# Norms and gates that read the matmul's PSUM bank directly, in a two-layer decoder trunk on one core

## The chip, the cores and the metric

The kernel runs on one core of one Trainium2 chip. The core has five engines that run side by side, each through its own queue of instructions: TensorE (PE in the profile; its weight loads are listed as PEld), VectorE (DVE), ScalarE (ACT), GpSimd (POOL) and SyncE (SP), which issues the DMAs. Matmuls write PSUM, which has eight banks of 128x512 float32; VectorE and ScalarE read PSUM, GpSimd in this kernel works on SBUF only.

The metric is the time of one execution in device microseconds, the median of several runs. Lower is better.

## The reference

Two residual layers over 1024 tokens of width 1024. Each layer normalises its input, projects it with one wide weight matrix, runs three mixers on slices of the projection, multiplies each mixer's output by its own gate, and projects back:

```python
h = rms_norm(x, ln_g[layer])
u = h @ w_in[layer]                       # even: 2,744 columns, odd: 3,504
y1, y2, y_m = mixers(split_cols(u))       # even: latent attention | sparse block attention | memory attention
                                          # odd:  indexer-selected attention | mLSTM | memory attention
mix = concat([y1 * silu(gate1), y2 * silu(gate2), y_m * silu(gate_m)])
x = x + mix @ w_out[layer]
```

Almost every slice of `u` that becomes a query or a key is normalised head by head before use: `rms_norm(q) = q * rsqrt(mean(q*q) + 1e-6) * g`. In the indexer-selected attention each query attends to the 256 keys with the highest index scores; the index scores come from eight small index queries per token. For the first 256 tokens every earlier key is among the 256, so their index queries decide nothing.

## The kernel before

All work is on tiles of 128 tokens (`NT = 8`). A float32 matrix product is made of three float16 products of high and low halves (`mm3`, line 1061). The float16 halves of a weight block are scaled by a power of two; undoing that scale is a multiplication by a per-partition column `wi[:, 0:1]` (`winv` in the profile), which every consumer of a projection does while it copies the result from PSUM.

- `load_w` (979) loads a weight block in pages, squares each page for a sum (`wj`, `wss`), adds the pages' sums with a reduction (`wst`), sums over partitions with a float32 matmul against a matrix of ones, and derives the power-of-two scale. It then makes the halves `wl`.
- `project` (1071) runs over the blocks of a layer and the eight tiles: 24 matmuls per tile and block of up to 512 columns into one PSUM bank (`psO`), then a `post` function on that bank.
- A normalising `post` (`q_post`, `k_rope`, `post_lat`, `mem_post`, `kv_post` of `mla_kv`, `q_post` of `mla_q`, `post_idx`) makes two passes over the bank: a scaled copy into SBUF (tiles `qu`, `ku`, `lu`, `mqu`, `kvk`, `xu`) and a ScalarE square with the same scale. The rest uses SBUF: VectorE sums the squares, `rstd` (785) makes mean plus epsilon, GpSimd raises it to the power -0.5 (`rsqrt`, 781), and a multiply applies it to the copy. That multiply goes through `tt` (777), which may run on VectorE or GpSimd.
- A gate (`gate_post`, 1334; `post_og`, 2157) makes a tanh (`gth`, `ogt`) and a scaled copy (`gu`, `ogu`), both from the bank, and `silu` (1346) combines them on VectorE: (tanh + 1) * copy.

Nothing of this runs in program order. A recorder notes every operation with its dependencies; a planner (`order`, line 303) then lists, for each engine, the order in which its operations are issued. Operations are ranked by a key: each section of the program has an interval in the table `SEG`, and its operations are spread over that interval. Operations recorded through `copy` may run on ScalarE or VectorE, those through `tt` on VectorE or GpSimd (in the odd or out-projection parts a few other sets). The planner gives such an operation to the engine with the smallest estimated finish, in which `PRICE` weights each engine's duration (line 356):

```python
fin = {x: max(te[x], ready(o, x), shared(o, x), room) + alt[3] * (1 + PRICE[x]) for x, alt in o.alts.items()}
```

It also hands out the eight PSUM banks, which attention (`psS`, two banks for a unit of scores; `psT`, `psO`) shares with the projections. Attention per unit of work: scores into PSUM, a maximum (`nm`, VectorE), the exponential (`P` or `psum`, ScalarE), a split into two float16 halves (`PS` or `PT`: a scaled copy on either engine, then a subtraction on VectorE), a transpose by DMA or TensorE, and the product with the values.

Of the kernel before, what the change touches and what calls it, by code (L numbers as in the profile page):

```python
# [25 lines left out]
PRICE = {"V": 0.0, "S": 0.0, "G": 0.0}  # L26
# [636 lines left out]
def shape_constants():  # L663
# [8 lines left out]
    for i in range(NT):  # L672
# [8 lines left out]
SEG = dict(setup=(-1576.69593, -601.132494), mem1=(-688.598351, 20.410205), e_agate=(30.600801, 726.724683), norm=(40.663363,  # L681
           43.886871), kv0=(144.84029, 484.056211), late=(244.088906, 537.79462), cmp=(419.157656, 678.361546), nsak=(441.736796,
           1111.702063), nsav=(473.744964, 852.150721), q1=(516.97553, 589.82681), e_kv1=(657.175124, 658.175124), e_lat=(663.1,
           841.289575), q0=(716.011325, 958.711325), e_bgate=(717.414855, 785.212098), kv1=(721.080648, 931.480648), e_bq=(743.2,
           988.9), e_mq=(765.062608, 934.79172), e_kv2=(784.700952, 841.5), nsa=(850.7, 1310.2), mla0=(911.5, 1001.5),
           mla1=(949.844544, 1032.244544), mem0=(995.320402, 1196.998026), tab1=(998.505496, 1809.787053), oA0=(1017.297313,
           1145.595371), mkv0=(1037.7, 1137.062), oBM0=(1117.135472, 1369.183228), o_idx=(1295.192627, 1405.371644),
           topk0=(1315.598497, 1922.144632), o_og1=(1337.144784, 1596.707927), o_cgate=(1397.764817, 1813.702265),
           topk1=(1438.6657, 1890.616024), o_og0=(1538.232471, 1831.481071), o_dqk=(1661.136623, 1731.218797), o_mq=(1698.247094,
           1772.209632), o_cq=(1740.832086, 1897.126292), mlstm=(1752.857474, 2015.6), o_dv=(1791.594452, 1899.65152),  # L690
           mkv1=(1795.136495, 1846.39911), cv=(1864.304863, 1962.048226), dsa=(1918.765321, 2334.316374), oBM1=(1988.164978,
           2223.083031), oA1=(2187.593261, 2496.721847))
# [13 lines left out]
class Trunk:  # L706
    def __init__(self, tc, A, out, ctx):
# [19 lines left out]
        self.rec = rec = Recorder(LIMITS)  # L727
        self.real = dict(V=nc.vector, S=nc.scalar, G=nc.gpsimd, T=nc.tensor, Q=nc.sync)
        self.V, self.S, self.G, self.T, self.Q = (Engine(rec, n, self.real[n]) for n in "VSGTQ")

    soft = False
# [63 lines left out]
    def setup(self):  # L795
# [12 lines left out]
        V.memset(self.ones, 1.0)  # L808
        self.gmax = self.const([128, 6], F, "gmax")
# [169 lines left out]
    def load_w(self, parts, nk, gain=None, fuse=False):  # L979
# [91 lines left out]
    def project(self, layer, blocks, hT, gain):  # L1071

        for name, (parts, post) in blocks.items():
# [260 lines left out]
    def gate_post(self, dst, o=0):  # L1334
# [11 lines left out]
    def silu(self, out, th, u):  # L1346

        if self.soft:
            self.tt(th, th, u, OP.mult, "G")
# [1161 lines left out]
```

## Time and profile before

| | |
|---|---|
| median of 3 runs | 1514.36 us (1513.29 to 1518.81) |
| the profiled execution | 1524.7 us, of it 1522.9 us from the first to the last instruction |
| TensorE | 1397.5 us busy, 92%; granted clock 0.957 of full speed on average |
| VectorE | 1355.0 us, 89% |
| ScalarE | 1061.1 us, 70% |
| GpSimd | 380.2 us, 25% |

The profile cuts the span into stretches and gives each engine's busy time in each. Every operation carries one line number, that of the recorder's issue loop (L559), so groups are told apart by the names of the tiles they write and read: `qu<-psum,winv` is the scaled copy of a query block, `qu<-qu,ms` the multiply by the reciprocal root. A granted clock of 1.00 is 2.4 GHz, 0.50 is 1.2 GHz.

### The profile page before, as it was taken

To read this page: it belongs to the slowest core of one execution; us is meant where nothing else is said; L and a number is where in the kernel's file an instruction comes from. 1 tells how busy PE (TensorE), PEld (TensorE's weight loads), DVE (VectorE), ACT (ScalarE), POOL (GpSimd) and SP (SyncE) were. 2 spreads that over 40 slices of the span, in tenths; PEclk is the share of its full clock that TensorE was granted. 3 is DMA by queue.
4 is the path that set the end of the run, shared out by engine and by line. 5 is a ranking of instruction groups with operands and counts; after the bars stand their busy time and mean duration, and the time that the engine had idled before them with its cause. 6 is when DMAs were issued, how large, how long until landed. Compare 5 with 4: busy or idle time off the path is not lost. (4 is left out here: it accounts for less than half of the span.)

```text
span 1522.9 us, 29899 instructions
## 1 busy us (share of the span) xinstructions
PE 1397.5 (92%) x10407; PEld 796.4 (52%) x10407; DVE 1355.0 (89%) x3681; ACT 1061.1 (70%) x2460; POOL 380.2 (25%) x436
## 2 busy tenths in 40 slices
PE   4999999979898889979999999999989898999988
PEld 1445446546666555655565544444444445655554
DVE  7867989899999898899999989779999999799994
ACT  6733855578876787786777679999889824456561
POOL 1411344557520123341114100001222121210110
PEclk9999999989999999989999999999998899689999
DMA  9847222367884889878987404013242645459994
GB/s 295 198 147 173 94 82 84 92 150 165 142 175 103 188 198 235 229 165 176 231 194 167 116 23 139 15 56 97 67 125 80 129 87 170 112 133 263 266 222 142
DMA packets 441847, 225.47 MB, mean 148 GB/s; under 512 B 378080, under 2 KB 404320, under 8 KB 441696
## 3 DMA queue, kind: packets, MB, share of 16 engines
q1 hardware_dynamic: 441696, 223.57, 59.6%
q8 instruction: 81, 1.33, 0.4%
q14 instruction: 70, 0.57, 0.1%
HBM read 83.61 MB, written 46.66 MB: 86 GB/s over the span
## 5 line engine op out<-in xcount | busy, mean ns | idle before, releaser
L559 PE MATMUL psum<-wl,hT 128*128 128x512 f16 (+3 forms) x2880 | 680.9, 372 | 11.9 <-DVE wl L559 4.3
L559 PEld LDWEIGHTS <-hT 128*128 128x128 f16 x2880 | 276.9, 99 | 307.4 <-issue 34.2
L559 PEld LDWEIGHTS <-PT 128*128 128x128 f16 x3792 | 248.4, 103 | 66.4 <-DMA PT<-PS 27.1
L559 PE MATMUL psum<-wl,oT 128*128 128x512 f16 x960 | 273.8, 385 | 3.3 <-DMA oT<-osp 0.9
L559 POOL TENSOR_TENSOR ms<-ms,nhalf 128x4 f32<-128x4 f32 (+3 forms) x105 | 113.9, 1092 | 435.0 <-DVE ms L559 335.1
L559 PE MATMUL psum<-nv,PT 128*128 128x64 f16 x1584 | 183.3, 193 | 11.3 <-DMA PT<-PS 6.4
L559 ACT ACTIVATE psum<-psum,nm 128x256 f32<-128x256 f32 (+8 forms) x234 | 137.4, 591 | 68.1 <-DVE nm L559 53.4
L559 DVE TENSOR_REDUCE nm<-psum 128x2 f32<-128x512 f32 (+8 forms) x216 | 162.4, 764 | 19.7 <-PE psum L559 18.9
L559 PEld LDWEIGHTS <-oT 128*128 128x128 f16 x960 | 93.9, 99 | 100.3 <-issue 8.1
L559 ACT ACTIVATE P<-psum,nm 128x64 f32<-128x64 f32 (+8 forms) x150 | 92.4, 623 | 57.7 <-DVE nm L559 46.0
L559 DVE SCALAR_TENSOR_TENSOR PS<-psum,PS 128x512 f16<-128x512 f32 (+6 forms) x160 | 124.1, 783 | 2.5 <-ACT PS L559 2.4
L559 PE MATMUL psum<-cst,P 128*128 128x128 f32 x502 | 107.3, 299 | 10.9 <-DVE PS L559 6.8
L559 PEld LDWEIGHTS <-qf 128*128 128x128 f16 x832 | 78.6, 103 | 66.4 <-issue 23.1
L559 PE MATMUL psum<-cvp,PT 128*128 128x64 f16 x864 | 106.1, 200 | 5.6 <-DMA PT<-PS 5.6
L559 ACT ACTIVATE PT<-psum 128x512 f16<-128x512 f32 (+3 forms) x160 | 77.4, 505 | 45.4 <-PE psum L559 40.2
L559 PE MATMUL psum<-nkst,qf 128*128 128x320 f16 (+5 forms) x384 | 93.5, 322 | 3.9 <-DVE PS L559 2.1
L559 DVE TENSOR_TENSOR wl<-wr,wl 128x1024 f16<-128x1024 f32 (+4 forms) x76 | 92.8, 1230 | 0.8 <-ACT wl L559 0.5
L559 ACT ACTIVATE tkj<-tkr,tkv 128x384 bf16<-128x384 f32 (+5 forms) x96 | 83.8, 879 | 13.5 <-DVE tkv L559 7.5
L559 DVE SCALAR_TENSOR_TENSOR PT<-psum,PT 128x512 f16<-128x512 f32 (+3 forms) x160 | 88.2, 566 | 5.3 <-ACT PT L559 5.2
L559 PEld LDWEIGHTS psum<-cst,P 128*128 128x128 f32 x502 | 68.2, 145 | 31.0 <-DVE PS L559 7.6
L559 ACT ACTIVATE wj<-wr 128x1024 bf16<-128x1024 f32 (+6 forms) x73 | 74.1, 1020 | 13.7 <-DMA wr<-even_w_in 7.7
L559 ACT ACTIVATE tkj<-stop,tkd,tkf 128x768 bf16<-128x768 bf16 (+5 forms) x84 | 80.8, 970 | 0.4 <-DVE tkb L559 0.4
(508 smaller groups left out, 2896.1 us busy)
## 6 DMA issues: line engine op xcount, KB each, us to landing
wr<-even_w_in SPq DMA_DIRECT2D x20, 512.0 KB, 5.7
wr<-w_out SPq DMA_DIRECT2D x20, 512.0 KB, 5.4
wr<-odd_w_in SPq DMA_DIRECT2D x20, 512.0 KB, 4.3
gate<-gate_d SPq DMA_DIRECT2D x32, 256.0 KB, 4.2
gate_d<-gu SPq DMA_DIRECT2D x24, 256.0 KB, 2.1
qa_d<-mqT SPq DMA_DIRECT2D x16, 384.0 KB, 2.5
xt<-x SPq DMA_DIRECT2D x8, 512.0 KB, 9.9
x<-x SPq DMA_DIRECT2D x8, 512.0 KB, 5.3
```

Of the source, the lines that this page charges most:

```text
L559: r = getattr(engines[o.eng], meth)(*[res(a) for a in args], **{k: res(v) for k, v in kw.items()})
```

## The change

Four kinds of edits. First, the normalising posts and the gates no longer make the scaled copy: the square is taken of the unscaled bank, the epsilon is divided by the square of the scale (`eps_of`, two small VectorE operations per weight block), and the multiply reads the bank and runs on VectorE alone. The gates' scale is kept (`gw`) and multiplied once into a small per-head factor of the attention that the gate will multiply. Second, the weight sums go to the ones matmul in bfloat16, page by page. Third, for the first two token tiles the index projection leaves out the 256 columns of the index queries, in two column ranges instead of one. Fourth, `PRICE` and the table `SEG` have new numbers.

```diff
-PRICE = {"V": 0.0, "S": 0.0, "G": 0.0}
+PRICE = {"V": 0.715, "S": -0.1744, "G": 0.0874}
 ...
-SEG = dict(setup=(-1576.69593, -601.132494), mem1=(-688.598351, 20.410205), e_agate=(30.600801, 726.724683), ...
+SEG = dict(mem1=(-1888.036415, -777.253203), setup=(-1705.34707, -1400.274884), e_agate=(29.974308, 702.674675), ...
 ...
-    def rstd(self, ss, n, scale=1.0):
+    def rstd(self, ss, n, scale=1.0, eps=None):
         ms = self.tiny(ss.shape[-1], F, "ms")
         c2 = 1.0 / (scale * scale)
-        self.V.tensor_scalar(ms, ss, c2 / n, EPS * c2, op0=OP.mult, op1=OP.add)
+        self.V.tensor_scalar(ms, ss, c2 / n, EPS * c2 if eps is None else eps, op0=OP.mult, op1=OP.add)
         return self.rsqrt(ms)
+
+    def eps_of(self, w, c2=1.0):
+
+        key = (id(w.t), str(w.ops), c2)
+        if key not in self.epss:
+            e = self.tiny(2, F, "eps")
+            self.V.reciprocal(e[:, 0:1], w)
+            self.V.tensor_scalar(e[:, 1:2], e[:, 0:1], e[:, 0:1], EPS * c2, op0=OP.mult, op1=OP.mult)
+            self.epss[key] = (w, e[:, 1:2])
+        return self.epss[key][1]
 ...
-        tot = ss
-        if npg > 1:
-            tot = self.tiny(1, F, "wst")
-            V.tensor_reduce(out=tot, in_=ss, axis=AX.X, op=OP.add)
+        tot = self.tiny(npg, BF, "wst")
+        V.tensor_copy(tot, ss)
         gcols, gmax = self.gcols[gain]
         t = self.psT()
-        T.matmul(t[:, 0:1], self.ones, tot, start=True, stop=True)
+        for p in range(npg):
+            T.matmul(t[:, 0:1], self.oneb, tot[:, p:p + 1], start=p == 0, stop=p == npg - 1)
 ...
-                    self.mm3(ps[:, :n], [(hi[:, k], lo[:, k]) for k in range(8)], w)
+                    for a, b in (((0, 128), (384, n)) if name == "idx" and i < 2 else ((0, n),)):
+                        self.mm3(ps[:, a:b], [(hi[:, k], lo[:, k]) for k in range(8)], [(x[:, a:b], y[:, a:b]) for x, y in w])
 ...
-            th, u = self.page("gth", [128, n]), self.page("gu", [128, n])
-            self.S.activation(th, ps[:, o:o + n], AF.Tanh, scale=wi[:, 1:2])
-            self.copy(u, ps[:, o:o + n], scale=wi[:, 0:1])
-            self.silu(u, th, u)
+            if i == 0:
+                self.gw[name] = g = self.const([128, 1], F, "gw")
+                self.V.tensor_copy(g, wi[:, 0:1])
+            u = self.page("gu", [128, n])
+            self.S.activation(u, ps[:, o:o + n], AF.Tanh, scale=wi[:, 1:2])
+            self.silu(u, u, ps[:, o:o + n])
 ...
-        def norm_heads(u, sq, h, d, n, scale=1.0):
+        def norm_heads(u, src, sq, wi, h, d, n, scale=1.0):
+
+            S.activation(sq, src, AF.Square)
             ss = self.tiny(h, F, "nh")
-            V.tensor_reduce(out=ss, in_=sq.rearrange("p (h d) -> p h d", h=h), axis=AX.X, op=OP.add)
-            r = self.rstd(ss, n, scale)
-            u3 = u.rearrange("p (h d) -> p h d", h=h)
-            self.tt(u3, u3, self.bc(r, [128, h, d], 2), OP.mult)
-            return u3
+            h3 = lambda x: x.rearrange("p (h d) -> p h d", h=h)
+            V.tensor_reduce(out=ss, in_=h3(sq), axis=AX.X, op=OP.add)
+            r = self.rstd(ss, n, scale, self.eps_of(wi[:, 0:1], 1.0 / (scale * scale)))
+            V.tensor_tensor(out=h3(u), in0=h3(src), in1=self.bc(r, [128, h, d], 2), op=OP.mult)
+            return h3(u)
 ...
-                self.copy(u, ps, scale=wi[:, 0:1])
-                S.activation(sq, ps, AF.Square, scale=wi[:, 0:1])
-                u3 = norm_heads(u, sq, 8, 64, 64, 0.125)
+                u3 = norm_heads(u, ps, sq, wi, 8, 64, 64, 0.125)
 ...
+        V.tensor_scalar(inv, inv, self.gw["a"], None, op0=OP.mult)
 ...
+        for f in (cmp["inv"], vsi, vwi):
+            V.tensor_scalar(f, f, self.gw["b"], None, op0=OP.mult)
 ...
-                self.copy(u[:, 0], ps[:, 256:512], scale=wi[:, 0:1])
-                self.silu(u[:, 0], th[:, 1], u[:, 0])
+                self.silu(u[:, 0], th[:, 1], ps[:, 256:512])
                 self.silu(u[:, 1], th[:, 0], u[:, 0])
                 x3 = u[:, 1].rearrange("p (h d) -> p h d", h=2)
-                self.tt(x3, x3, hg, OP.mult)
+                V.scalar_tensor_tensor(out=x3, in0=x3, scalar=wi[:, 0:1], in1=hg, op0=OP.mult, op1=OP.mult)
```

`mem_post`, `k_rope`, `post_lat`, `kv_post`, `mla_q` and `post_idx` are changed in the way of `q_post` and `norm_heads`. `post_lat` makes its two float16 halves straight from the bank. All 36 intervals of `SEG` are new; the sections stay in much the same order, except that `mem1` now comes ahead of `setup`, `tab1` starts at 830 (998 before), `topk1` starts at 1272 (1439 before) and lies ahead of `topk0`.

## Rows read from the trace of the kernel before

**Rows 1.** Busy time by stretch: start:end, length, engines (instructions), clock, DMA share, GB/s
```profile
core 0: us, PE busy (x) PEld busy (x) DVE busy (x) ACT busy (x) POOL busy (x), PEclk, DMA share, GB/s
50.00:300.00 250.00, 249.99 (x1307) 130.25 (x1306) 208.04 (x757) 138.24 (x302) 89.78 (x89) 1.00 0.40 121
300.00:550.00 250.00, 212.93 (x2427) 147.41 (x2426) 237.85 (x546) 186.59 (x528) 95.41 (x129) 0.94 0.72 152
550.00:700.00 150.00, 131.96 (x1331) 85.17 (x1331) 138.96 (x311) 119.45 (x295) 53.05 (x51) 0.93 0.88 210
700.00:850.00 150.00, 144.49 (x1387) 89.29 (x1386) 142.37 (x334) 108.21 (x248) 33.98 (x56) 1.00 0.86 186
850.00:1000.00 150.00, 146.43 (x715) 70.35 (x714) 125.46 (x351) 132.33 (x259) 7.32 (x13) 0.99 0.24 76
1000.00:1150.00 150.00, 143.81 (x675) 67.11 (x673) 140.48 (x391) 136.25 (x285) 29.02 (x19) 0.99 0.30 86
1150.00:1350.00 200.00, 180.16 (x1096) 107.09 (x1096) 180.71 (x509) 116.66 (x312) 43.42 (x46) 0.84 0.46 115
1350.00:1500.00 150.00, 141.76 (x1281) 80.09 (x1280) 130.34 (x325) 85.36 (x176) 17.29 (x18) 0.98 0.96 230
```

**Rows 2.** Waits of TensorE, 300 to 550 us: who waited for whom, us, times, longest
```profile
PE psum L559 <- DVE PS L559: 10.1, 11, 2.3
PE psum L559 <- DMA PT<-PS: 7.7, 8, 1.9
PE psum L559 <- DVE PT L559: 4.0, 5, 1.6
PE psum L559 <- ACT P L559: 4.0, 3, 2.6
```

**Rows 3.** TensorE in order of time: start, us from first to last, instruction, count
```profile
809.90 0.90 PE L559 MATMUL psum<-wl,hT 128*128 128x432 f16 x4
1389.94 0.54 PE L559 MATMUL psum<-cvp,PT 128*128 128x64 f16 x13
43.14 0.28 PE L559 MATMUL psum<-wst,ones 128*128 128x1 f32 x2
43.28 0.92 PE L559 MATMUL psum<-wl,hT 128*128 128x512 f16 x3
```

**Rows 4.** Groups of scaled copies, whole span: count, busy us, mean ns, idle before
```profile
L559 DVE TENSOR_SCALAR gu<-psum,winv 128x512 f32<-128x512 f32 (+1 forms) x16 | 10.3, 644 | 2.8 <-PE psum L559 2.8
...
L559 DVE TENSOR_SCALAR qu<-psum,winv 128x512 f32<-128x512 f32 x3 | 2.2, 734 | 0.0
L559 ACT ACTIVATE gu<-psum,winv 128x512 f32<-128x512 f32 (+1 forms) x24 | 14.3, 597 | 2.3 <-DVE kvs L559 2.3
...
L559 ACT ACTIVATE xu<-psum,winv 128x416 f32<-128x416 f32 x4 | 2.4, 606 | 2.8 <-PE psum L559 2.8
```

**Rows 5.** Groups of multiplies and splits, whole span
```profile
L559 POOL TENSOR_TENSOR mqn<-mqu,mqms 128x256 f32<-128x256 f32 x4 | 2.6, 658 | 0.2
L559 DVE TENSOR_TENSOR mqn<-mqu,mqms 128x256 f32<-128x256 f32 x12 | 5.0, 414 | 0.7 <-POOL mqms L559 0.7
L559 DVE TENSOR_TENSOR mixA<-psum,cf 128x256 f32<-128x256 f32 x32 | 13.4, 418 | 4.3 <-PE psum L559 4.0
L559 DVE TENSOR_SCALAR gu<-psum,winv 128x256 f32<-128x256 f32 x6 | 2.9, 476 | 0.0
L559 DVE TENSOR_SCALAR lsp<-lu,lms 128x256 f16<-128x256 f32 x6 | 2.1, 346 | 0.0
L559 DVE TENSOR_REDUCE wst<-wss 128x1 f32<-128x4 f32 (+2 forms) x21 | 3.1, 146 | 1.9 <-ACT wj L559 1.9
```

**Rows 6.** Groups of movable operations on VectorE, 300 to 700 us, then 1150 to 1350
```profile
L559 DVE TENSOR_SCALAR PS<-psum 128x512 f16<-128x512 f32 (+6 forms) x34 | 27.9, 826 | 0.8 <-ACT psum L559 0.6
L559 DVE TENSOR_TENSOR wl<-wr,wl 128x1024 f16<-128x1024 f32 x9 | 11.5, 1274 | 0.2 <-ACT wl L559 0.2
L559 DVE TENSOR_SCALAR PS<-psum 128x512 f16<-128x512 f32 (+1 forms) x13 | 8.5, 663 | 0.5 <-ACT psum L559 0.5
L559 DVE TENSOR_TENSOR wl<-wr,wl 128x1024 f16<-128x1024 f32 x8 | 10.2, 1280 | 0.0
```

**Rows 7.** One query tile at 1258 us, in order of time: start, us, instruction, [idle before]
```profile
1258.14 0.70 ACT L559 ACTIVATE qsq<-psum,winv 128x512 f32<-128x512 f32 x1
1263.46 2.61 POOL L559 TENSOR_TENSOR ms<-ms,nhalf 128x8 f32<-128x8 f32 x2 [5.41 <-DVE ms L559]
1265.13 0.69 DVE L559 TENSOR_TENSOR qu<-qu,ms 128x512 f32<-128x512 f32 x1
```

More of the change, by code (lines that the diff above doesn't have):

```diff
@@ L678, in shape_constants @@
     return c
[L681 to L692, printed above, removed]
@@ new lines @@
+SEG = dict(mem1=(-1888.036415, -777.253203), setup=(-1705.34707, -1400.274884), e_agate=(29.974308, 702.674675), norm=(66.196882,
+           67.196882), kv0=(119.873601, 326.461801), late=(271.705755, 580.746202), nsak=(334.268778, 1740.215819),
+           cmp=(368.353292, 488.762377), nsav=(434.363812, 870.544721), q1=(475.175395, 617.189084), q0=(566.735709, 931.932049),
+           e_kv1=(660.555602, 663.443172), e_lat=(663.187987, 829.025091), e_bgate=(705.954963, 783.352092), kv1=(726.464295,
+           936.864295), e_bq=(737.259234, 982.959234), e_mq=(765.062608, 932.900552), e_kv2=(784.700952, 841.5), tab1=(830.090423,
+           1662.888056), nsa=(872.306006, 1326.817021), mla0=(909.091866, 999.091866), mla1=(969.44378, 1054.709671),
+           oA0=(1007.713145, 1135.977063), mkv0=(1040.445181, 1139.807181), mem0=(1079.69846, 1246.165943), oBM0=(1120.434423,
+           1372.482179), topk1=(1271.85213, 1873.537022), o_idx=(1296.691587, 1402.187939), topk0=(1324.470154, 1930.279265),
+           o_og1=(1349.453914, 1536.855486), o_cgate=(1379.693649, 1771.670217), o_og0=(1514.069868, 1768.540855),
+           o_dqk=(1600.358214, 1661.086999), o_mq=(1713.3677, 1855.898155), o_cq=(1753.414658, 1888.851314), o_dv=(1783.429201,
+           1908.616007), mlstm=(1817.611125, 2013.865219), cv=(1830.061497, 1982.44894), mkv1=(1844.716227, 1889.690991),
+           dsa=(1892.935508, 2303.398001), oBM1=(1962.41115, 2241.424255), oA1=(2195.850639, 2403.005228))
@@ L1346, in silu @@
     def silu(self, out, th, u):
-        if self.soft:
-            self.tt(th, th, u, OP.mult, "G")
-            self.tt(out, th, u, OP.add, "G")
-        else:
-            self.V.scalar_tensor_tensor(out=out, in0=th, scalar=1.0, in1=u, op0=OP.add, op1=OP.mult)
+        self.V.scalar_tensor_tensor(out=out, in0=th, scalar=1.0, in1=u, op0=OP.add, op1=OP.mult)
     def mem_kv(self, l):
@@ L1564, in post_lat @@
             pg = ptab[0]
-            u, sq = self.page("lu", [128, 416]), self.page("lsq", [128, 416])
-            self.copy(u, ps[:, 0:416], scale=wi[:, 0:1])
-            S.activation(sq, ps[:, 0:416], AF.Square, scale=wi[:, 0:1])
+            sq = self.page("lsq", [128, 416])
+            S.activation(sq, ps[:, 0:416], AF.Square)
             ss = self.tiny(3, F, "lss")
@@ L1573, in post_lat @@
             V.tensor_tensor(out=ms, in0=ss, in1=self.cst[:, C_MEAN:C_MEAN + 3], op=OP.mult)
-            V.tensor_scalar(ms, ms, EPS, None, op0=OP.add)
+            V.tensor_scalar(ms, ms, self.eps_of(wi[:, 0:1]), None, op0=OP.add)
             r = self.rsqrt(ms)
@@ L1734, in kv_post @@
             V.tensor_reduce(out=ss, in_=s4, axis=AX.X, op=OP.add)
-            r = self.rstd(ss, 64)
-            self.tt(k4, k4, self.bc(r, [128, 4, 64], 2), OP.mult)
+            r = self.tiny(4, F, "ms")
+            V.tensor_scalar(r, ss, bq[:, 1:2], self.eps_of(wk), op0=OP.mult, op1=OP.add)
+            self.rsqrt(r)
+            V.tensor_tensor(out=k4, in0=p4[:, :, 0:64], in1=self.bc(r, [128, 4, 64], 2), op=OP.mult)
             ks = self.split_rows(k4, "kvs")
@@ L1775, in q_post @@
         def q_post(i, ps):
-            u, sq = self.page("mqu", [128, 384]), self.page("mqs", [128, 384])
-            n = self.page("mqn", [128, 384])
-            self.copy(u, ps, scale=wi[:, 0:1])
-            S.activation(sq, ps, AF.Square, scale=wi[:, 0:1])
-            u4, s4 = h4(u), h4(sq)
+            sq, n = self.page("mqs", [128, 384]), self.page("mqn", [128, 384])
+            S.activation(sq, ps, AF.Square)
+            p4, s4 = h4(ps), h4(sq)
             ms = self.tiny(8, F, "mqms")
@@ L2003, in post_idx @@
             wv = wi[:, 0:1]
-            self.copy(u1[:, 0:416], ps[:, 0:416], scale=wv)
             self.copy(cv[:, i], ps[:, 64:128], scale=wv)
-            V.tensor_scalar(iw[:, i], ps[:, 416:424], wv, float(np.float32(8.0 ** -0.5)), op0=OP.mult, op1=OP.mult)
+            if i >= 2:
+                self.copy(u1[:, 128:416], ps[:, 128:416], scale=wv)
+                V.tensor_scalar(iw[:, i], ps[:, 416:424], wv, float(np.float32(8.0 ** -0.5)), op0=OP.mult, op1=OP.mult)
+            else:
+                self.copy(u1[:, 384:416], ps[:, 384:416], scale=wv)
             V.tensor_scalar(gif[:, i], ps[:, 424:432], wv, None, op0=OP.mult)
             sq = self.page("xsq", [128, 64])
-            S.activation(sq, ps[:, 0:64], AF.Square, scale=wv)
-            k3 = self.norm_heads(u1[:, 0:64], sq, 1, 64, 64)
+            k3 = self.norm_heads(u1[:, 0:64], ps[:, 0:64], sq, wi, 1, 64, 64)
             r = self.page("xr", [128, 8, 128])
@@ L2229, in dsa @@
         groups = []
+        V.tensor_scalar(vinv, vinv, self.gw["c"], None, op0=OP.mult)
         ql = self.q_load(cq_d, 128, 8)
```

51 lines of the change are left out of this document (27 added, 24 removed).

## The prediction

> **What bounds the kernel now.** I read the page first (TensorE 92% busy, VectorE 89%, ScalarE 70%, GpSimd 25%), then the busy time by stretch, since an average over stages hides which engine is the limit in each. [rows 1] show two kinds of stage. From 50 to 300 us TensorE is busy 249.99 of 250 us at clock 1.00: the projections of the even layer, bound by TensorE. From 700 to 1150 us it is busy 144 to 146 of 150 at clock 0.99 to 1.00: nearly so. From 300 to 700 us and from 1150 to 1350 us VectorE is the fullest engine (237.85 + 138.96 + 180.71 = 557.5 of 600 us), while TensorE is busy 525 of 600, and part of that at half clock: its clock of 0.94, 0.93 and 0.84 means that (0.06 x 250) + (0.07 x 150) + (0.16 x 200) = 57 us of full-speed work are lost, so at full clock it would need some 468 of 600. These 600 us are where VectorE's time counts. ScalarE is busy 423 of them, GpSimd 192. Who ends TensorE's waits there [rows 2]: VectorE 14.1 us (`PS`, `PT`), DMA 7.7, ScalarE 4.0. So VectorE ends 55% of the waits shown, no more.
>
> **The change part by part.**
>
> **Index columns.** Two tiles x 24 = 48 matmuls of 432 columns become 48 of 128 and 48 of 48. A run of four of 432 columns lasts 0.90 us from first start to last end [rows 3]; one lasts 0.35 by itself (the profile's matmul durations include the pipeline), so their spacing is about 0.55/3 = 0.183 us. Thirteen matmuls of 64 columns, each with a weight load of its own, last 0.54 us, 0.19 of it the last one's pipeline: 0.35/12 = 0.029 us apart. Then 128 columns cost 0.183 x 128/432 = 0.054, and the 48 no more than 0.029. Saved: 48 x (0.183 - 0.083) = **4.8 us**. The tiles lie near 810 us, in a stretch where TensorE is 96% busy, so I count all of it; bounds 0 and 4.8.
>
> **Weight sums.** The two passes of the float32 sum hold TensorE for 0.14 us: they start at 43.14, the next projection matmul at 43.28 [rows 3]. Four bfloat16 matmuls at 0.029 make 0.12. With 21 sums that is 0.5 us. The copy takes the place of a reduction of 146 ns [rows 5]. I count **0**.
>
> **The scaled copies.** On VectorE there are seven groups that I could see, from `gu` (10.3 us) to `qu` (2.2) [rows 4], 30 us, of which `xu` keeps two thirds: some 29 us go. On ScalarE eight groups from `gu` (14.3) to `xu` (2.4) make 52.6 us, and 51 go. But nearly all of them follow projections, and those run where TensorE is full. Of VectorE's 29 us only about 4 lie in the 600 us that it bounds. The other 25, and the ScalarE time, are hidden by matmuls and are worth nothing in their own place: **-4 us** of VectorE time that counts.
>
> **The multiplies** become VectorE's alone. GpSimd ran 13 of them; in VectorE's durations (0.658 becomes 0.414 us for 256 columns [rows 5]) they add some 5.7 us, all but three in 300 to 550 us: **+5 us**. Reading PSUM costs nothing extra: 418 ns for `mixA<-psum,cf` against 414 for the same size from SBUF [rows 5]. The single-source split of `post_lat` is another matter: 346 ns from SBUF for 256 columns, 476 ns for a scaled read of PSUM of that size, so up to 0.13 us more for each of its copies on VectorE, 11 of them, all at 125 to 290 us under full matmuls: 0.
> The Trainium skill (VectorE: DVE Perf Modes, Rules for kernel authors) speaks against the change: results of a matmul are to be taken at the slow rate, or copied to SBUF first if many operations follow. The trace bears out the slower single-source read and not a slower two-input one; by that rule the sum would be 11 x 0.13 = 1.4 us worse, in a place that matmuls hide.
>
> **Small operations.** Some 12 epsilons of two operations, 6 copies and 8 small products of the gates' scales, and a few in `mla_kv`: about 42 x 0.15 us (the 146 ns reduction is the nearest row) = 6 us of VectorE, half of it where it counts: **+3 us**. So the direct reads by themselves do nothing for the stages that VectorE bounds: -4 + 5 + 3 = **+4 us**.
>
> **PRICE.** This is what can move those stages. A VectorE duration now counts 1.715, ScalarE's 0.826, GpSimd's 1.087. A copy of 0.8 us goes to ScalarE unless that is some 0.7 us further behind; an add goes to GpSimd if VectorE is a little later, though GpSimd takes 1.6 times as long (658 against 414 ns [rows 5]). What VectorE does there and may give away, in the largest groups [rows 6]: the `PS` copies 27.9 + 8.5 = 36.4 us, the `wl` subtractions 21.7 us; many smaller groups come to about as much again. I take half of the copies (18 us), a quarter of the subtractions (5) and the same share, 17, of the small groups: **-40 us**. The bounds are 0 (the planner already sent copies to the engine that was free) and -70. ScalarE has 177 us free there, GpSimd 408.
>
> **The order.** `SEG` is new, but the sections' sequence is nearly the old one. I can't cost it from rows; it lies within +10 and -15 us, and I take 0.
>
> **The sum.** VectorE time in its 600 us: -40 + 4 = -36 us. Of that the share of the waits that VectorE ends is gained, 0.55 x 36 = 20 us; then DMA landings, ScalarE's exponentials and TensorE itself are next late. With 4.8 us of index columns: 25 us; I take off 2 for longer chains through GpSimd. -23 us on an execution of 1524.7, span 1522.9, gives 1501.7; scaled to the median of the runs (1514.36/1524.7 = 0.993), -23 us: **1491 us**.
>
> **The rivals.**
> *More of it.* All 36 us and more turn into time, as VectorE is 93% busy there and the 25 us freed before 300 us let attention begin earlier. For: TensorE needs only 468 of 600. Against: [rows 2]. 50 us gained: 1465.
> *Nothing.* The planner already balanced the engines, PRICE moves little, and what the copies free lies under full matmuls. For: [rows 1] and the place of the copies. Then the index columns' 4.8 us are left, less some small operations: 1511. That the change does not do what it says has the same result.
> *Slower: PSUM banks.* A bank was free after the last of two passes; now it is held until the multiply. In [rows 7] the square ends at 1258.84, the multiply at 1265.82: seven microseconds more, through VectorE's queue and GpSimd's power, and a fuller GpSimd makes them more. From 50 to 300 us projections have the eight banks nearly to themselves. From 300 to 550 and 1150 to 1350 us attention shares them, and I find 15 and 4 such tiles there. If a hold meets eight taken banks, TensorE's next group waits for up to 7 us. Four such stalls (28 us) use up the gain; from five on it is slower. At six, 42 - 25 = 17 us lost: 1531. Against: the planner knows the banks and can put other work ahead; [rows 2] name no wait for a bank.
>
> **How the numbers follow.** The forecast (1477 to 1504) has 0.50, more of it 0.16, nothing 0.19, slower 0.15. The low end 1464 takes in nearly all of "more of it", the high end 1523 "nothing" and the near edge of the slower case; about 0.17 is left out. The likeliest case's own range is 1477 to 1504. A measurement of this kernel can tell about 0.5% (7.6 us) from no change: faster 0.66, same 0.19, slower 0.15.
>
> **What would show it.** Right: VectorE's total falls to about 1290 us and ScalarE's does not rise; the `PS` copies on VectorE fall from 47 in the 600 us to about half; the stretch from 300 to 700 us gets shorter while 50 to 300 stays; GpSimd's total rises by 30 us or more. The index matmuls should show 48 of 128 and 48 of 48 columns. Wrong: TensorE waits before projection groups on `qu`, `mqu` or `gu` (banks); `PS` copies stay on VectorE; or the time moves in a stretch that none of this touches, which would be the new order's doing.

## The result, and the profile after

The changed kernel takes 1508.31 us (median of 20 runs, 1503.38 to 1512.84), the kernel before, run beside it, 1517.86 us (1506.84 to 1523.21). The ratio is 0.9943, with a 95% interval of 0.9929 to 0.9957: **8.7 us faster** by the ratio (the medians are 9.6 apart), where 23 were forecast. The profiled executions are 16.9 us apart (span 1506.0 against 1522.9), which overstates it: the one of before took 1524.7 us, 6.8 more than the median of its kernel.

The totals of after, from the page (engine, busy us, share of the span, instructions):

```profile
PE 1375.8 (91%) x10496; PEld 790.1 (52%) x10496; DVE 1271.5 (84%) x3530; ACT 1084.5 (72%) x2500; POOL 411.2 (27%) x447
```

VectorE lost 83.5 us of its 1355.0. But TensorE was not busy for 1522.9 - 1397.5 = 125.4 us before and for 1506.0 - 1375.8 = 130.2 after: **its waiting did not get shorter.** What fell is its busy time, by 21.7 us. Of that, up to 12.8 is the granted clock, by an estimate: at a mean clock of 0.957 the profiled execution of before lost 0.043 x 1522.9 = 65.5 us of full-speed time, after (0.965) it lost 52.7, and a part of either fell in TensorE's idle time. The index columns are 4 to 5 us (below).

Busy time by stretch, after, to be laid beside [rows 1]:

```profile
50.00:300.00 250.00, 249.11 (x1311) 128.82 (x1310) 190.51 (x707) 141.61 (x313) 113.25 (x130) 1.00 0.43 128
300.00:550.00 250.00, 217.92 (x2490) 147.99 (x2489) 237.50 (x550) 197.41 (x545) 88.06 (x111) 0.99 0.80 161
550.00:700.00 150.00, 130.93 (x1343) 84.23 (x1342) 123.21 (x271) 116.96 (x283) 41.01 (x38) 0.94 0.89 196
1150.00:1350.00 200.00, 175.45 (x1148) 109.53 (x1147) 170.94 (x478) 112.15 (x304) 51.55 (x46) 0.82 0.53 117
```

In the 600 us of the forecast VectorE is busy 237.50 + 123.21 + 170.94 = 531.7 us (557.5 before), TensorE 524.3 (525.1). From 300 to 550 us VectorE is as full as it was (237.85 before).

TensorE's waits of after, 300 to 550 us, to be laid beside [rows 2]:

```profile
PE psum L559 <- DMA PT<-PS: 6.2, 9, 1.3
PE psum L559 <- ACT P L559: 5.8, 9, 1.2
PE psum L559 <- DVE PT L559: 5.4, 8, 1.2
PE psum L559 <- DVE PS L559: 5.0, 9, 1.4
PE psum L559 <- DVE mqn L559: 2.4, 1, 2.4
PE psum L559 <- ACT PT L559: 2.4, 5, 0.8
PE psum L559 <- DVE mqu L559: 1.2, 2, 0.7
```

The waits that `PS` ends were halved, from 10.1 to 5.0 us. Others took the place of most of that: `PT` 4.0 to 5.4, ScalarE's `P` and `PT` 4.5 to 8.2, and two names that are new here, `mqn` and `mqu`, 3.6 us: the multiplies that now read the bank. Before, the next rows below [rows 2] were waits of this kind too, for the copy and the square that read the bank then:

```profile
PE psum L559 <- ACT gu L559: 2.5, 1, 2.5
PE psum L559 <- ACT mqs L559: 2.0, 1, 2.0
```

TensorE is not busy for 37.1 us of this stretch before and 32.1 after; from 550 to 700 us it is 18.0 and 19.1, from 1150 to 1350 us 19.8 and 24.6, so over the 600 us nothing is won.

The groups of after that answer to [rows 5, 6], whole span:

```profile
L559 DVE TENSOR_SCALAR PS<-psum 128x640 f16<-128x640 f32 (+4 forms) x17 | 11.9, 699 | 1.6 <-PE psum L559 1.1 <-ACT psum L559 0.5
L559 ACT ACTIVATE PS<-psum 128x512 f16<-128x512 f32 (+6 forms) x143 | 101.1, 717 | 2.6 <-DMA xq_d<-x 1.7
L559 POOL TENSOR_TENSOR wl<-wr,wl 128x1024 f16<-128x1024 f32 (+3 forms) x22 | 46.8, 2130 | 224.2 <-DMA wr<-odd_w_in 170.7 <-ACT wl L559 31.8 <-DVE wl L559 21.8
L559 DVE TENSOR_TENSOR mqn<-psum,mqms 128x256 f32<-128x256 f32 x16 | 6.7, 416 | 2.9 <-POOL mqms L559 2.6
L559 DVE CAST wst<-wss 128x4 bf16<-128x4 f32 (+3 forms) x25 | 4.0, 159 | 4.8 <-ACT wj L559 4.8
L559 PE MATMUL psum<-wl,hT 128*128 128x432 f16 x144 | 38.4, 348 | 0.0
L559 PE MATMUL psum<-wl,hT 128*128 128x128 f16 x48 | 5.9, 219 | 0.0
L559 PE MATMUL psum<-wl,hT 128*128 128x48 f16 x48 | 3.2, 183 | 0.0
```

`PRICE` did what it says: of 160 `PS` copies VectorE keeps 17 (59 before), GpSimd makes 22 `wl` subtractions (12 before).

**Where the time left.** Two marks split the span: the start of the first index score (`relu` on ScalarE) and the start of the last selection mask (`dmask` on VectorE). Before the first lie the even layer and the odd projections up to it, between them the top-k search with the mLSTM and the odd projections, behind the second the selected attention and the last output projection.

Starts of these tiles, before:

```profile
L559 ACT ACTIVATE relu<-psum x42: 487/771/1040, 836.0 to 946.6; 128x384 f32<-128x384 f32 x7, 128x512 f32<-128x512 f32 x7, 128x640 f32<-128x640 f32 x7, 128x768 f32<-128x768 f32 x7
L559 DVE TENSOR_SCALAR dmask<-tkg x6: 247/334/414, 1231.3 to 1274.6; 128x768 bf16<-128x768 bf16 x1, 128x896 bf16<-128x896 bf16 x1, 128x384 bf16<-128x384 bf16 x1, 128x1024 bf16<-128x1024 bf16 x1
```

and after:

```profile
L559 ACT ACTIVATE relu<-psum x42: 467/760/1031, 834.2 to 916.7; 128x384 f32<-128x384 f32 x7, 128x512 f32<-128x512 f32 x7, 128x768 f32<-128x768 f32 x7, 128x896 f32<-128x896 f32 x7
L559 DVE TENSOR_SCALAR dmask<-tkg x6: 248/334/411, 1141.9 to 1255.3; 128x768 bf16<-128x768 bf16 x1, 128x896 bf16<-128x896 bf16 x1, 128x1024 bf16<-128x1024 bf16 x1, 128x384 bf16<-128x384 bf16 x1
```

The even part takes 836.0 us before and 834.2 after, the search part 438.6 and 421.1, the tail 248.3 and 250.7. By these marks all of the gain lies in the middle, and the even part, where the forecast expected most of it (300 to 700 us), is as long as it was. The busy times of the three parts, before:

```profile
0.00:836.00 836.00, 753.21 (x6486) 456.79 (x6486) 755.13 (x2040) 582.98 (x1416) 280.04 (x333) 0.97 0.70 168
836.00:1274.60 438.60, 414.16 (x2133) 204.65 (x2132) 395.32 (x1103) 348.07 (x750) 66.89 (x68) 0.97 0.30 84
1274.60:1522.90 248.30, 230.15 (x1792) 134.92 (x1790) 204.58 (x540) 130.01 (x296) 33.27 (x35) 0.90 0.78 196
```

and after:

```profile
0.00:834.20 834.20, 747.06 (x6599) 452.37 (x6600) 703.83 (x1953) 600.02 (x1445) 285.39 (x340) 0.98 0.74 169
834.20:1255.30 421.10, 397.84 (x2054) 199.83 (x2051) 370.56 (x1035) 345.22 (x740) 87.32 (x76) 0.96 0.33 87
1255.30:1506.00 250.70, 230.95 (x1847) 137.89 (x1846) 197.07 (x545) 139.26 (x315) 38.50 (x32) 0.92 0.80 191
```

In the even part **VectorE is busy 51.3 us less and the time is 1.8 us shorter**; TensorE is not busy for 82.8 us before and 87.1 after. The marks don't cut equal work: of TensorE's 2133 instructions in the search part 2054 are left. Some 40 projection matmuls now stand ahead of the first mark, and some 48 of the mLSTM behind the second. The search part is shorter by 16.3 us of TensorE's busy time and 1.1 us of its waiting, so its gain is in part work that the new order put elsewhere.

### The profile page after: what moved, and what is told of

It is laid out like the page before. It is cut to its first block, busy times and chain, and to the rows that moved or that the text cites. A ratio compares the mean times of both kernels' runs of the same rounds, so it can differ in the third digit from the quotient of the medians.

```text
span 1506.0 us, 30045 instructions
## 1 busy us (share of the span) xinstructions
PE 1375.8 (91%) x10496; PEld 790.1 (52%) x10496; DVE 1271.5 (84%) x3530; ACT 1084.5 (72%) x2500; POOL 411.2 (27%) x447
## 4 chain that ended last, share of the span: by engine, by line
PE 45%; DVE 26%; ACT 12%; DMA 9%; issue 5%; POOL 2%; SPq 1%; DVEq 0%; ACTq 0%; POOLq 0%
PE psum L559 45%; ACT tkj L559 6%; DMA PT<-PS 6%; DVE nm L559 3%; DVE PS L559 2%; DVE wl L559 2%; ACT psum L559 2%; DVE PT L559 2%; DMA wr<-mem_w_kv 1%; DVE psum L559 1%; POOL ms L559 1%; SPq L559 1%; DVE tkr L559 1%; DMA gate<-gate_d 1%; ACT P L559 1%
## 5 line engine op out<-in xcount | busy, mean ns | idle before, releaser
L559 PE MATMUL psum<-wl,hT 128*128 128x512 f16 (+4 forms) x2928 | 656.8, 365 | 9.0 <-DMA hT<-nh 3.8
L559 PEld LDWEIGHTS <-PT 128*128 128x128 f16 x3792 | 240.0, 102 | 68.8 <-DMA PT<-PS 31.1
L559 PE MATMUL psum<-nv,PT 128*128 128x64 f16 x1584 | 172.0, 194 | 15.3 <-DMA PT<-PS 9.2
L559 DVE TENSOR_REDUCE nm<-psum 128x1 f32<-128x640 f32 (+8 forms) x216 | 161.8, 765 | 17.7 <-PE psum L559 16.2
L559 PE MATMUL psum<-cst,P 128*128 128x128 f32 x502 | 103.3, 296 | 9.5 <-ACT P L559 4.4
L559 POOL TENSOR_TENSOR wl<-wr,wl 128x1024 f16<-128x1024 f32 (+3 forms) x22 | 46.8, 2130 | 224.2 <-DMA wr<-odd_w_in 170.7
L559 PE MATMUL psum<-cvp,PT 128*128 128x64 f16 x864 | 99.1, 196 | 5.8 <-DMA PT<-PS 4.4
L559 ACT ACTIVATE PS<-psum 128x512 f16<-128x512 f32 (+6 forms) x143 | 101.1, 717 | 2.6 <-DMA xq_d<-x 1.7
L559 DVE SCALAR_TENSOR_TENSOR PT<-psum,PT 128x512 f16<-128x512 f32 (+3 forms) x160 | 88.0, 566 | 10.6 <-ACT PT L559 10.1
L559 ACT ACTIVATE wj<-wr 128x1024 bf16<-128x1024 f32 (+5 forms) x82 | 84.6, 1034 | 11.7 <-DMA wr<-even_w_in 5.3
L559 ACT ACTIVATE tkj<-tkr,tkv 128x512 bf16<-128x512 f32 (+5 forms) x96 | 83.4, 871 | 7.7 <-DVE tkv L559 6.8
```

Of the source, the lines that this page charges most:

```text
L559: r = getattr(engines[o.eng], meth)(*[res(a) for a in args], **{k: res(v) for k, v in kw.items()})
```

## The experiments

All ratios are to the kernel before, run on the same chip beside them, with 95% intervals; 0.001 is 1.5 us.

**One part, or all but one.** The kernel before with the new `PRICE`:

```diff
-PRICE = {"V": 0.0, "S": 0.0, "G": 0.0}
+PRICE = {"V": 0.715, "S": -0.1744, "G": 0.0874}
```

> The kernel before with the new PRICE alone (old SEG, scaled copies as before). Theory A (the forecast's: VectorE's time bounds 300 to 700 and 1150 to 1350 us, PRICE relieves it): VectorE's total falls by 40 us or more and the time by 15 to 20 us (ratio 0.987 to 0.990). Theory B (VectorE is busy there but what ends last is TensorE's own work and the chains between engines): VectorE's total falls as much and the time stays within 0.5%.

Measured: 1.0285 (1.0238 to 1.0332). VectorE's total fell to 1311.1 us and ScalarE's rose to 1124.9, so the work moved as intended, and the kernel got 43 us slower, which neither theory had expected.

The changed kernel with both old tables (reads, weight sums and index columns alone):

```diff
-PRICE = {"V": 0.715, "S": -0.1744, "G": 0.0874}
+PRICE = {"V": 0.0, "S": 0.0, "G": 0.0}
-SEG = dict(mem1=(-1888.036415, -777.253203), ...
+SEG = dict(setup=(-1576.69593, -601.132494), ...
```

> The direct reads, bfloat16 sums and shorter index projection alone (old PRICE, old SEG). Theory A: VectorE's total falls by about 20 us, ScalarE's by 40, nearly all under full matmuls; the time falls by the 5 us of the index columns (ratio 0.996 to 0.998). Rival C (PSUM banks held until the multiply): TensorE waits before projections and the time rises by 0.5% or more.

Measured: 1.0216 (1.0171 to 1.0261). That is the time that the rival of the banks would give, but TensorE waits only 8.0 us in all for operations that now read a bank, most of it once, where the kernel is 33 us slower:

```profile
PE psum L559 <- DVE mqu L559: 6.5, 1, 6.5
```

VectorE's total is 1353.6 us, hardly below the 1355.0 of before, where 20 less were expected; ScalarE's is 1013.0, 48 less (40 were expected).

The kernel before with the new `SEG`:

```diff
-SEG = dict(setup=(-1576.69593, -601.132494), ...
+SEG = dict(mem1=(-1888.036415, -777.253203), ...
```

> The new SEG table alone on the kernel before. Theory A gives it no weight: ratio 0.995 to 1.005. Rival D (the new order is what gains or loses): a ratio outside of that, with the time moved in stretches where the sections were moved.

Measured: 1.0359 (1.0324 to 1.0395), 55 us slower, outside the bounds that the prediction gave the order (+10 and -15).

The changed kernel with the old `SEG` only:

```diff
-SEG = dict(mem1=(-1888.036415, -777.253203), ...
+SEG = dict(setup=(-1576.69593, -601.132494), ...
```

> All of the change but the new SEG table. Theory A: as the forecast, 20 us or more faster (ratio below 0.987). Theory B: within 0.5% of the kernel before. If this is faster than the whole change (ratio below 0.994), the new order gave back what the rest had gained.

Measured: 1.0197 (1.0158 to 1.0236). Every part by itself is slower, and so is the change without its order. This pointed at how well a table fits the operations that it orders: the order's fit.

**Order nudged a little.** Every interval of `SEG` is shifted by at most 2 of its units (the table reaches from -1577 to 2497), on both kernels; the operations and `PRICE` stay. The two further pairs have 7 and 5 in place of 3. The offsets go by the place in the table (`j`), and the two tables list their sections in different orders, so the sections of a pair are not shifted alike:

```diff
+SEG = {k: (a + ((j * 37 + 3) % 11 - 5) * 0.4, b + ((j * 37 + 3) % 11 - 5) * 0.4)
+       for j, (k, (a, b)) in enumerate(SEG.items())}
```

> The kernel before with every interval of SEG shifted by a fixed small amount of at most 2 units (the table spans some 4,000). No operation, cost or duration changes, only the listed order. Theory E (the table of an earlier search fits one set of operations only; any other order costs 2 to 4%, whatever the edit): ratio 1.01 or more, most of it before the top-k begins. Rival A or B (the edits themselves made the runs so far slower): within 0.5% of 1.

> The whole change with every interval of its SEG shifted by at most 2 units in the same way. Theory E: the time rises to 1.01 or more of the kernel before, as in the runs with a table that was made for another set. Rival: it stays near the whole change's 0.994, and then the new operations are worth something with any order near this one.

> The kernel before with its SEG intervals shifted by at most 2 units in a second pattern. Theory E (the table was fitted to this set of operations and the loss is that of any other order): again 1.02 to 1.04. A ratio within 0.5% would say that the first pattern was unlucky and the order is worth little.

> The whole change with its SEG intervals shifted by at most 2 units in a second pattern. Theory E: 1.005 to 1.02 of the kernel before. If edits are worth some 20 to 30 us with orders that fit neither set, this and the first pattern lie that much below the nudged kernels before (1.03).

> The kernel before, with each interval of SEG shifted by another set of offsets of at most 2 units. If 3.2% is what the kernel before loses when its order is only nearly the fitted one (nudges 1 and 2: 1.0324 and 1.0331), this gives 1.028 to 1.038. If those two were bad luck, anything from 1.000 to 1.02.

> The whole change, with the same offsets as in the third nudge of the kernel before. If the edits are worth some 20 to 30 us wherever the order is not fitted, this is 0.013 to 0.022 below the third nudge of the kernel before, near 1.008 to 1.018. If the edits are worth no more than the 9 us of the result, it is within 0.008 of that kernel.

Measured, in this order: 1.0324 (1.0285 to 1.0364) and 1.0099 (1.0065 to 1.0133); 1.0331 (1.0299 to 1.0363) and 1.0165 (1.0140 to 1.0191); 1.0229 (1.0178 to 1.0279) and 1.0109 (1.0071 to 1.0147). A shift that means nothing costs the kernel before 2.9% on average and the kernel after 1.0124/0.9943 = 1.8%. Between kernels of nudged order the edits, the two new tables among them, are worth 2.2, 1.7 and 1.2% of the time of before: **on average 1.7%, some 26 us, near the 23 of the forecast**; between the two kernels as they are, 0.57%.

A nudge is not the order alone. The planner chooses the engines as it lists the operations, and under the three nudges it gives VectorE 1378.2, 1374.1 and 1369.8 us in the kernel before (1355.0 un-nudged), 1276.8, 1275.3 and 1274.8 in the kernel after (1271.5). So the nudged kernels differ by 98 us of VectorE's time, the un-nudged by 83.5.

The totals of one such pair, the second nudge of before:

```profile
PE 1411.6 (90%) x10407; PEld 803.9 (51%) x10407; DVE 1374.1 (87%) x3725; ACT 1057.5 (67%) x2447; POOL 370.3 (24%) x405
```

and of after:

```profile
PE 1396.6 (90%) x10496; PEld 801.0 (52%) x10496; DVE 1275.3 (83%) x3492; ACT 1081.9 (70%) x2523; POOL 402.3 (26%) x462
```

Their spans are 1574.6 and 1544.0 us: TensorE is not busy for 163.0 and 147.4 us. Here the waiting does get shorter. All eight profiles, split at the two marks, in us (one profile each for the first two rows):

| | even part | search part | tail | TensorE not busy | TensorE busy |
|---|---|---|---|---|---|
| before | 836.0 | 438.6 | 248.3 | 125.4 | 1397.5 |
| after | 834.2 | 421.1 | 250.7 | 130.2 | 1375.8 |
| before, nudged (mean of 3) | 867.6 | 442.3 | 258.3 | 162.7 | 1405.5 |
| after, nudged (mean of 3) | 850.8 | 427.8 | 261.5 | 146.8 | 1393.3 |

In the search part, with the marks as they are, the edits gain 15 to 18 us in either row pair. In the even part they gain 17 us under nudged orders and 2 under the kernels' own: the order of before is 32 us better there than its neighbours, that of after 17 us.

**The tables mixed.** The kernel after with the old `PRICE`, and the kernel before with both new tables:

```diff
-PRICE = {"V": 0.715, "S": -0.1744, "G": 0.0874}
+PRICE = {"V": 0.0, "S": 0.0, "G": 0.0}
```

> The direct reads, weight sums, index columns and the new SEG, with the old PRICE (all zero). The engine choice then differs from the one that the new SEG came with. If the order's fit is what decides, this lies with the nudges of the whole change: 1.008 to 1.02. If the new SEG is good whatever the prices, it is near the whole change: 0.992 to 1.000. If PRICE is most of the gain by itself, it is 1.02 or more.

> The kernel before with the new PRICE and the new SEG together, its operations unchanged (scaled copies kept). If the two new tables are good for any such kernel once they stand together, this is near the whole change: 0.995 to 1.005. If they serve only the operations that they came with, it lies with the other mixed kernels: 1.02 to 1.04.

Measured: 1.0342 (1.0302 to 1.0382), as expected if `PRICE` were most of the gain, and 1.0173 (1.0117 to 1.0230), between the two expectations. But `PRICE` alone gave no gain above (1.0285). All eight mixtures of the three parts are now there:

| | old tables | new PRICE | new SEG | both new |
|---|---|---|---|---|
| old operations | 1 | 1.0285 | 1.0359 | 1.0173 |
| new operations | 1.0216 | 1.0197 | 1.0342 | 0.9943 |

The parts don't add. With the old tables the new operations cost 2.2%; with both new tables they gain 1.0173 - 0.9943 = 2.3%. With the new operations `PRICE` gains 0.2% under the old `SEG`, which is within the intervals, and 4.0% under the new one. Without `PRICE` the new operations leave VectorE 1353.6 us (old `SEG`) and 1352.7 (new), so nearly all of the 83.5 us that VectorE lost came with `PRICE`.

**VectorE's copies given to ScalarE.** In the kernel before, the order is left as planned, and at issue all 59 `PS` copies of VectorE go to ScalarE:

```diff
+            if o.eng == "V" and "S" in o.alts and o.alts["V"][1] and o.alts["V"][1][0].t.name.startswith("PS_"):
+                o.eng = "S"
```

> The kernel before, planned as before; then, as the operations are issued in the planned order, all 59 PS copies of VectorE (47.6 us) go to ScalarE instead, each at its place in the order. That is PRICE's largest effect without a new order. Theory A (VectorE's time bounds the even layer): 10 us or more faster. Theory B (time that VectorE is busy there is not what ends last): within 0.5%; ScalarE's queue may make it slower.

Measured: 1.0036 (1.0008 to 1.0064). All 160 copies are ScalarE's:

```profile
L561 ACT ACTIVATE PS<-psum 128x512 f16<-128x512 f32 (+6 forms) x160 | 109.7, 697 | 2.4 <-ACT oj L561 0.5 <-ACT PT L561 0.4 <-PE psum L561 0.2
```

The stretches of this kernel:

```profile
300.00:550.00 250.00, 211.27 (x2437) 147.07 (x2436) 227.87 (x529) 197.23 (x549) 94.35 (x129) 0.95 0.71 153
550.00:700.00 150.00, 129.32 (x1323) 83.10 (x1322) 127.14 (x293) 126.98 (x307) 53.85 (x51) 0.94 0.90 207
1150.00:1350.00 200.00, 181.04 (x1082) 106.39 (x1081) 174.88 (x504) 124.45 (x330) 41.66 (x45) 0.83 0.43 115
```

In the 600 us VectorE is busy 529.9 in place of 557.5, and nothing is gained. Over the span its total fell to 1318.6 us, by 36.4 (the copies' 47.3 us overlap their neighbours in the profile). But the copies did not leave the chain of their tiles: VectorE subtracts the same tile behind each copy, and now it waits for ScalarE. The subtractions, before and here:

```profile
L559 DVE SCALAR_TENSOR_TENSOR PS<-psum,PS 128x512 f16<-128x512 f32 (+6 forms) x160 | 124.1, 783 | 2.5 <-ACT PS L559 2.4
```

```profile
L561 DVE SCALAR_TENSOR_TENSOR PS<-psum,PS 128x512 f16<-128x512 f32 (+6 forms) x160 | 125.0, 787 | 25.9 <-ACT PS L561 23.6 <-issue 0.9 <-ACT PT L561 0.2
```

Of the freed time 21.2 us came back as VectorE's waiting for the copies. So the run shows that **handing these copies to ScalarE, the largest thing that `PRICE` does, pays nothing at this order**; it doesn't show what VectorE's time would be worth if the work were gone altogether. The Trainium skill (Perfetto Trace Analysis, Identifying the Most-Contended Engine) says to optimise the engine of the highest occupancy first. By busy time VectorE is that engine in these 600 us (557.5 us, TensorE 525.1); the run neither bears the rule out nor speaks against it, as the chain kept its steps.

Time added instead: one VectorE reduction of 0.68 us after every 29th (after) or 31st (before) operation of VectorE, 119 and 116 of them, order unchanged:

```diff
 ...
+                if nv % 29 == 0:
+                    engines["V"].tensor_reduce(out=jout, in_=junk, axis=AX.X, op=OP.max)
```

> The whole change in its own order, with a reduction of 128x512 (some 0.68 us) that nothing needs put behind every 29th VectorE operation: some 120 of them, 83 us, as much VectorE time as the change took away. Theory A (VectorE's time bounds 600 us at 0.55): 18 us or more slower than the whole change, ratio above 1.006. Theory B (VectorE's time is not the bound): 10 us or less, ratio 0.994 to 1.001.

> The kernel before, its own order, with one reduction of about 0.68 us put on VectorE after every 31st of its operations, spread evenly (about 80 us more VectorE time), as was done to the whole change (where it cost 32 us, 2.1%). If VectorE is the engine on whose time the kernel before hangs more than that of the kernel after (it is busier by 83 us), the cost is larger: 1.025 to 1.05. If what counts is only that a fixed order meets later producers, the cost is the same: 1.018 to 1.025. If VectorE's time is not on the path, under 1.007.

The group in the changed kernel:

```profile
L566 DVE TENSOR_REDUCE junkout<-junkin 128x1 f32<-128x512 f32 x119 | 80.4, 675 | 0.0
```

Measured: 1.0155 (1.0130 to 1.0180), which is 1.0155/0.9943 = 2.1% or 32 us above the whole change; and 1.0240 (1.0188 to 1.0293), 36 us. The reductions' 80 us overlap other operations too: VectorE's total rises by 59.3 us (to 1330.8) and by 56.3 (to 1411.3). So a microsecond of added busy time cost some 0.54 and 0.65 us. That is on the forecast's side of what was expected (18 us or more), near its 0.55, while moving copies away gave nothing. The cost in the busier kernel is as expected if it is no more sensitive, though its interval reaches into the other case. How much of these costs is VectorE's time, and how much only that a planned order met other durations, these two runs don't separate.

**Other engines' time.** In the kernel before, at the planned order, 2 of each projection group's 24 matmuls are left out (240 of 2880):

```diff
 ...
-            T.matmul(ps, al, bh, start=False, stop=(k == n - 1))
+            T.matmul(ps, al, bh, start=False, stop=(k == n - 1)).skip = k < less
```

> The kernel before in its own order, without 240 of the 2880 projection matmuls (two of the low-half products in each group of 24; part of the product is left out, so the output is less exact): 240 x 0.216 = 52 us less TensorE work, some 24 us of it in the even layer and 28 in the odd. Theory F (TensorE's own work bounds the stages of full matmuls): 15 to 25 us faster, nearly all before 300 us, since the odd layer's projections lie beside the top-k. Theory A: the same, since it took 50 to 300 us as bound by TensorE; less than 8 us would speak against both.

Measured: 0.9929 (0.9899 to 0.9959), 11 us. The 52 us expected of TensorE's work were by the matmuls' spacing; its busy time fell by 39.4, to 1358.1. Nearly all of the gain is in the even part (first score at 823.3 us in place of 836.0). The search part stays at 437.8, though TensorE is busy 12.9 us less there (401.25). The 11 us lie between what was expected if TensorE's own work bounds the full stages (15 to 25) and what would have spoken against it (under 8).

And the last 4 of the 16 levels of the search for the lower end of the threshold are left out at issue:

```diff
 ...
+                    if side == -1.0 if not isinstance(side, View) else False:
+                        for o in self.rec.ops[n0:]:
+                            o.skip = x >= len(bits) - 4
```

> The kernel before in its own order, with the last four of the 16 levels of the low-half top-k search left out as it is issued (that part of the computation is missing, so ties are cut less exactly): 4 of 31 levels for two groups of tiles. From the first sign to the last (919 to 1234 us) a pair of levels takes 315/31 = 10 us. Theory G (between the first index scores and the last mask the chain of the search is the bound, not TensorE): 25 to 40 us faster, all of it between the first score and the last mask. Theory F (the projections of the odd layer bound that stretch): less than 8 us, and more idle time on ScalarE.

Measured: 1.0006 (0.9982 to 1.0029). From 1150 to 1350 us ScalarE is busy 90 us in place of 116.7 [rows 1], and the time stays:

```profile
1150.00:1350.00 200.00, 184.26 (x1042) 108.86 (x1042) 168.42 (x447) 90.05 (x251) 37.83 (x42) 0.77 0.43 107
```

TensorE's busy time rose by 4 us there, at a clock of 0.77 in place of 0.84, so the lower clock may hide a small gain. Four levels less did not shorten the kernel, and fewer matmuls did not shorten the search part. What bounds that part stays open.

## Why the prediction was right or wrong

The direction was right, the size was not: -8.7 us against -23, close to the rival "nothing".

**Index columns: right.** 48 of 128 and 48 of 48 columns, as said. Their busy time is 5.9 + 3.2 = 9.1 us; 48 matmuls of 432 columns in this kernel's own rows take 48 x 38.4/144 = 12.8. That is 3.7 us by busy time, against 4.8 worked out from spacings. The spacings themselves hold: a run of 24 of 128 columns and 14 of 48 should last 24 x 0.054 + 14 x 0.029 = 1.70 us and the last one's 0.18 behind it, and lasts 1.85.

```profile
787.89 1.85 PE L559 MATMUL psum<-wl,hT 128*128 128x128 f16 x38
```

**Weight sums: no gain, as said.** The copy takes 159 ns (the reduction 146), and TensorE's waits that `wst` ends, over the whole span, did not get shorter. Before and after:

```profile
PE psum L559 <- DVE wst L559: 10.2, 2, 10.0
```

```profile
PE psum L559 <- DVE wst L559: 13.7, 3, 9.9
```

No run isolates these sums.

**Copies and multiplies: right in the price of one, not in the total.** A two-input multiply costs 416 ns from PSUM and 414 from SBUF [rows 5]. The sum took some 17 us off VectorE's total with the direct reads (-29 + 6 + 6); with the old tables they took off 1.4, as the planner gave VectorE other work (69 `PS` copies in place of 59). The rule of the Trainium skill that was weighed in the prediction (VectorE: DVE Perf Modes, Rules for kernel authors), to copy first if many operations follow, would save nothing for these two-input ones; the tier table of the same page (VectorE: DVE Perf Modes, The perf-mode tier table) has float32 two-input operations at the single rate from either memory, and the trace agrees.

**Small operations: counted too small.** The eps of `rstd` became a column where it had been a constant. That was not counted. Of before and after:

```profile
L559 DVE TENSOR_SCALAR ms<-nh 128x2 f32<-128x2 f32 (+2 forms) x40 | 6.2, 158 | 0.2
L559 DVE TENSOR_SCALAR mqms<-mqms 128x4 f32<-128x4 f32 x32 | 4.3, 159 | 0.0
```

```profile
L559 DVE TENSOR_SCALAR ms<-nh,eps 128x2 f32<-128x2 f32 (+2 forms) x40 | 9.8, 244 | 0.3
L559 DVE TENSOR_SCALAR mqms<-mqms,eps 128x4 f32<-128x4 f32 x32 | 6.7, 238 | 0.0
```

These 72 cost 6.0 us more; with 32 more of the same kind (`kvs`, `mqs`: 2.6 to 4.5 and 2.6 to 3.8 us) it is 9.1 us, on top of the 6 counted.

**PRICE: moved as much as forecast, and at these orders did not pay as forecast.** VectorE's total is 1271.5 (about 1290 was said), GpSimd's rose by 31.0 (30 or more), the `PS` copies in the 600 us fell from 47 to 13 (half was said). ScalarE's total rose by 23.4, where it was said not to rise: 42 more `PS` copies and 16 more `wl` copies (15.6 us) outweigh what the reads saved it. The failed step is the conversion: "the share of the waits that VectorE ends is gained, 0.55 x 36 = 20 us". VectorE's time in the 600 us fell by 557.5 - 531.7 = 25.8 us, and TensorE's time without work there went from 75.0 to 75.7. In the even part VectorE's fell by 51.3 us, and the part is 1.8 us shorter. From 300 to 550 us the waits that `PS` ended were mostly taken over by `PT`, ScalarE and the multiplies that hold the bank. And the copies given to ScalarE at a fixed order gave nothing, since VectorE then waited for them. A wait that an engine ends last is not time that it owes: when its work moves to another engine of the same chain, the chain keeps its length, and the next producer may be due right behind. The rate of 0.55 itself is not refuted: added VectorE time cost 0.54 and 0.65 of itself. What VectorE's time is worth when work disappears was not tried.

**The order: the term that was left at 0.** This is the second step that failed. It was taken as 0 since the sections' sequence is nearly the old one, with bounds of +10 and -15. More had moved than the text ahead of the prediction names: `nsak` now ends at 1740 (1112 before), and `cmp`, `q0`, `mem0` and `mlstm` have other neighbours too. Nudges with no purpose cost 1.2 to 3.6% (18 to 55 us: the outermost ends of the six intervals, those of after divided by 0.9943), and swapping the table alone 3.6%. So the order's term was wider than all the others, and any sum of durations says only what the change is worth between orders of equal fit. There the forecast's number was near: 26 us, of which the profiles show 16 as shorter waiting of TensorE (162.7 to 146.8). Its working is not shown by that: VectorE lost 98 us there, not 65, and the gain is in the search part as much as in the even one. That the two numbers meet may be luck. Shown is that both kernels sit on an order better than its three neighbours, and that of before by more: 2.9% against 1.8%. That this difference is why only 8.7 us are left is the arithmetic of these same numbers (26 - 17 = 9), not a further proof; whether the new operations have an order that is as good for them as the old one was for the old, was not tried.

**The rivals.** "Nothing" (1511) came nearest, for a reason it did not name: it said that `PRICE` moves little, and `PRICE` moved what was forecast. "More of it" had all of VectorE's freed time turn into gain; the even part shows none of it. "PSUM banks" appears in the waits of 300 to 550 us with 3.6 us at `mqn` and `mqu`, 3 waits, the longest 2.4 us, not six of 7. Over the whole span `gu` and `kvk` add 3.6 us, where `gu`, `mqs`, `ogt` and `ogu` had held TensorE for 6.0 before: these waits grew by about 1 us. The prediction's "[rows 2] name no wait for a bank" held only for the four rows shown. What was to be seen from 300 to 700 us did not happen; the time moved between 836 and 1275 us, where the sum counted VectorE only from 1150 on. There the old operations with both new tables already take 1283.7 - 857.3 = 426.4 us (their marks), so 12 of the 17.5 us need no direct reads. The new operations with `PRICE` and the old `SEG` take 1305.0 - 878.0 = 427.0, so as much needs no new `SEG`: the gain of this part can't be put down to one of the edits.

## What to carry to other kernels

Where every engine runs a queue in a planned order, first measure how much a meaningless shift of that order costs: if it is more than the edit is worth, compare the edit between several shifted orders of both kernels, and give the edit's worth and the order's fit as two numbers. Busy shares and the list of who ends the waits say where an engine is late, not what less of its work would give; that takes a run in which the work is taken away at the same order, and not handed to another engine of the same chain. Operations and planning tables that were changed together are to be judged together.

## What the runs showed of the hardware

- A VectorE operation on 2 to 4 elements takes 158 ns with two constants and 238 to 244 ns with a column from SBUF as its second scalar (groups above): some 80 ns for the column.
- A ScalarE square gets cheaper without its scale column: 527 to 435 ns for `mqs`, 686 to 591 for `qsq`. The Trainium skill (ScalarE: Activation LUTs, What ACT_TABLE_LOAD costs) states about 93 ns for each such column; the trace agrees. Before and after:

```profile
L559 ACT ACTIVATE qsq<-psum,winv 128x512 f32<-128x512 f32 x16 | 11.0, 686 | 1.0 <-DVE kvs L559 1.0
```

```profile
L559 ACT ACTIVATE qsq<-psum 128x512 f32<-128x512 f32 x16 | 9.4, 591 | 1.1 <-PE psum L559 1.1
```

- The spread of one kernel's times goes with TensorE's granted clock. Over the 57 executions of the kernel before, timed beside the experiments, the correlation of time and mean clock is -0.80, with 11 us for 0.01 of clock; which of the two brings on the other is not shown. The profiled execution of before had 0.957, the median of the 57 is 0.963: 0.006 of clock goes with some 7 us, so a part of the 16.9 us between the two profiles may be this spread.
